# Decays from a transposed broadcast column, with the mask applied on GpSimd, in a gated DeltaNet layer

## The chip, the core and the metric

The kernel runs on one core of a Trainium2 chip. The core has five engines that each take their instructions in program order and wait for one another by semaphores: TensorE (PE, with its weight loads shown as PEld), VectorE (DVE), ScalarE (ACT), GpSimd (POOL) and SyncE (SP), which here issues the large loads. SBUF is the on-chip memory, PSUM the smaller one that PE writes its products to. The metric is device time of one execution, in microseconds; a profile is a separate execution, recorded by the hardware.

## What is computed

One decoder layer over 256 tokens of width 2048: a gated DeltaNet mixer with 16 query/key heads and 32 value heads of 128, then a SwiGLU mixer, each with a modulation before and a layer norm behind it. The part that matters here builds, for each head, the matrix of decays between the positions of a chunk. `gc` is the running sum of the log gates.

```
gc = jnp.cumsum(g, -1)
diff = gc[..., :, None] - gc[..., None, :]
decay = jnp.where(lower, jnp.exp(jnp.where(lower, diff, 0.0)), 0.0)
L = jnp.where(strict, jnp.einsum('bhnid,bhnjd->bhnij', kb, k) * decay, 0.0)
sol = lax.linalg.triangular_solve(L + jnp.eye(C), rhs, left_side=True, lower=True, unit_diagonal=True)
a_qk = jnp.where(lower, jnp.einsum('bhnid,bhnjd->bhnij', q, k) * decay, 0.0)
```

So the products of keys with keys and of queries with keys are multiplied elementwise by exp(gc_i - gc_j), and entries where the key comes after the query are zero. The kernel keeps keys on the partitions and queries along the row, in chunks of 128, which is the same sum cut otherwise.

## The kernel before

All weights stream from device memory in loads of 512 KB. Each load (`raw`) is split into a high part `wh` on ACT (L190) and a low part `wl` on DVE (L191), and three matmuls of 128x512 (L223 to L225) give one product to fp32 precision; there are 6240 such big matmuls. PE works on them from start to end, and the small matmuls and transpositions of the DeltaNet mixer are put between them. The modulation's weights (`mraw`) are partly summed on DVE into `macc` (L272), and PE sums its partitions at L351.

The 32 heads are done in four quarters of eight. A quarter has these steps, all of them short tasks between big matmuls:

- four la tasks (`la_task`, two chunks times two groups of four heads), which make the decays and the masked products `LA`;
- `solve_task`: 62 small DVE operations in a chain (L584, L586) that solve the diagonal blocks, a DVE transposition into `XD` (L588), and products on PE from L600 on;
- two state tasks (`state_task`), which carry the state from the first chunk to the second, end with the products at L685, the sum `oq` on DVE (L686) and squares on ACT (L688);
- the norm of the quarter's output, `fo`: small DVE steps (L715 to L717), a power on POOL (L718), a DVE product (L719). It then scales the outputs `oq` at L795.

One la task works as follows. ACT makes four tiles `dg` that hold the column `gc` of a head in every column, plus `below`, a constant of -1e30 where the key comes after the query (L543). PE transposes them into one PSUM tile `pb` (L547), so that `gc` now runs along the row. ACT takes the exponential with minus `gc` as bias (L551) into `dm`. PE multiplies keys with keys and queries into a second PSUM tile `pk` (L556), and DVE multiplies `pk`, the scale `gsc` and `dm` into `LA` (L561). PSUM tiles `pb` and `pk` come from the pool `gd` with two buffers, which the state and solve tasks share; `dg` and `dm` come from the pool tag `V` with three.

The order of all work is set when the kernel is built. Each task is given a due time in units of some 24 big matmuls by `at`, `spawn` and the `yield` values (GDN, LAGAP, LA1 to LA3, SOLVE, HOP), and a scheduler then writes every engine's queue from these priorities. The engines keep to the queues. A quarter's la tasks begin after the quarter before has ended its state tasks.

Of the kernel before, what the change touches and what calls it, by code (L numbers as in the profile page):

```python
# [8 lines left out]
F32 = mybir.dt.float32  # L9
F32R = mybir.dt.float32r  # L10
I32 = mybir.dt.int32
AF = mybir.ActivationFunctionType
OP = mybir.AluOpType
# [16 lines left out]
def gdn_layer_kernel(ctx: ExitStack, tc: tile.TileContext, x, c, mod_w, mod_b, ln_g, ln_b,  # L30
                     w_gu, w_down, w_in, conv_w, a_log, dt_bias, norm_w, w_out, out):
    nc = tc.nc
# [2 lines left out]
    SPLIT, MOD0, MODEVERY = 10, 30.0, 0.95  # L35
    MGAP, CGAP0, CGAP, CSTEP = 1.5, 1.0, 2.0, 2.3
    CONV, PAIR, SILU = 0.2, 0.4, 2.4
    GDN, LAGAP, LA1, LA2, LA3, SOLVE, HOP = 3.0, 0.5, 0.3, 0.6, 1.5, 5.4, 0.6
    ALONE, MACW, ZW, OW = 1.5, 1.0, 0.1, 0.3


    consts = ctx.enter_context(tc.tile_pool(name="consts", bufs=1))
# [6 lines left out]
    act = nc.scalar.activation  # L49
    tt = nc.vector.tensor_tensor  # L50
    ts = nc.vector.tensor_scalar
    stt = nc.vector.scalar_tensor_tensor
    mm = nc.tensor.matmul
    tr = nc.tensor.transpose
# [35 lines left out]
    def tp():  # L90
        return psum.tile([128, 512], F32, name="tp", tag="tp", bufs=2)

    def gd():
        return psum.tile([128, 512], F32, name="gd", tag="gd", bufs=2)
# [17 lines left out]
    jp = work.tile([128, 128], I32, name="jp", tag="hf", bufs=2)  # L112
    nc.gpsimd.iota(jp, pattern=[[1, 128]], base=0, channel_multiplier=-1)
    ident = consts.tile([128, 128], F32, name="ident")
# [3 lines left out]
    ones = upper[:, 127:128]  # L118
    mhalf = consts.tile([128, 16], F32, name="mhalf")
    nc.vector.memset(mhalf, -0.5)  # L120
    below = consts.tile([128, 128], F32, name="below")
    ts(below, jp, 0.0, -1e30, op0=OP.is_gt, op1=OP.mult)

    pbit = work.tile([128, 1], I32, name="pbit", tag="gw0", bufs=1)
    nc.gpsimd.iota(pbit, pattern=[[0, 1]], base=0, channel_multiplier=1)
# [7 lines left out]
    p = tp()  # L133
# [16 lines left out]
    p = tp()  # L150
# [244 lines left out]
    gp = gp_ctx.__enter__()  # L395
# [6 lines left out]
    gc = consts.tile([128, 2, 32], F32, name="gc")  # L402
    ngc = consts.tile([128, 2, 32], F32, name="ngc")
# [132 lines left out]
    def la_task(q, c, g, sc):  # L536

        kqq, hv, la = kq[q], q * 8, LA[q]
        s0 = c * 8 + g * 4
        dg = gp.tile([128, 4, 128], F32, name="dg", tag="V", bufs=3)  # L540
        for i in range(4):
            h = hv + g * 4 + i
            act(dg[:, i, :], below, AF.Identity, bias=gc[:, c, h:h + 1])  # L543
        yield LA1
        pb = gd()
        for i in range(4):
            tr(pb[:, i * 128:(i + 1) * 128], dg[:, i, :], ident)  # L547
        dm = gp.tile([128, 4, 128], F32, name="dm", tag="V", bufs=3)
        for i in range(4):
            h = hv + g * 4 + i  # L550
            act(dm[:, i, :], pb[:, i * 128:(i + 1) * 128], AF.Exp, bias=ngc[:, c, h:h + 1])  # L551
        yield LA2
        pk = gd()
        for n in range(2):
            nn = g * 2 + n
            mm(pk[:, n * 256:(n + 1) * 256], kqq[:, nn, 0, c * 128:(c + 1) * 128],  # L556
               kqq[:, nn, :, c * 128:(c + 1) * 128], start=True, stop=True)
        for i in range(4):
            h = g * 4 + i
            src = pk[:, (i // 2) * 256:(i // 2 + 1) * 256].rearrange("p (a b) -> p a b", a=2)  # L560
            stt(la[:, s0 + i], src, sc[:, 0, c, h:h + 1], dm[:, i, None, :].to_broadcast([128, 2, 128]),  # L561
                op0=OP.mult, op1=OP.mult)

    def solve_task(q):

# [125 lines left out]
    def gdn(q):  # L691


        while q not in rq2 or q and q - 1 not in state_ends:
            yield 0.2
        hv, rk, rq = q * 8, rk2[q], rq2[q]
        LA[q] = gp.tile([128, 16, 2, 128], F32, name="LA", tag="LA", bufs=1)
        sc = work.tile([128, 2, 2, 8], F32, name="gsc", tag="gsc", bufs=2)
        tt(sc[:, 0], rk, rk, op=OP.mult)
        tt(sc[:, 0], sc[:, 0], beta[:, :, hv:hv + 8], op=OP.mult)  # L700
        tt(sc[:, 1, 0], sc[:, 0, 0], kse[:, hv:hv + 8], op=OP.mult)
        for c in range(2):
            for g in range(2):
                spawn(now[0] + LAGAP * (2 * c + g), la_task(q, c, g, sc))
        yield 3 * LAGAP + LA3
        yield from solve_task(q)
        omq[q] = work.tile([128, 2, 8], F32, name="om", tag="om", bufs=2)
        spawn(now[0] + 0.3, state_task(q, 1, sc))
        yield from state_task(q, 0, sc)
        while state_done.get(q) != 2:  # L710
            yield 0.1
        state_ends.add(q)
        f = work.tile([128, 2, 8], F32, name=f"fo{q}", tag=f"fo{q}", bufs=1)
        t = work.tile([128, 2, 8], F32, name="ft", tag="ft", bufs=1)
        tt(t, rq, rq, op=OP.mult)  # L715
        tt(t, t, omq[q], op=OP.mult)
        ts(t, t, 1.0 / 128.0, NORM_EPS, op0=OP.mult, op1=OP.add)  # L717
        nc.gpsimd.tensor_tensor(f.rearrange("p a b -> p (a b)"), t.rearrange("p a b -> p (a b)"), mhalf, op=OP.pow)  # L718
        tt(f, f, rq, op=OP.mult)  # L719
        fo[q] = f  # L720
# [298 lines left out]
    with tc.tile_pool(name="ph3", bufs=1, reuse_waits="tile") as p3:  # L1019
# [76 lines left out]
        for g in range(4):  # L1096
            if g == 1:
                for i, src in enumerate((ln_g, ln_b)):
                    for gg in range(4):
                        tag, n = ("sg", 2) if i and gg > 1 else ("an", 6)  # L1100
# [32 lines left out]
```

## Time and profile before

| | us |
| --- | --- |
| median of three runs | 1725.89 (1725.24 to 1726.46) |
| profiled execution | 1725.16 |
| its span, first to last instruction | 1723.4 |
| PE busy | 1668.0 (97%) |
| DVE busy | 1139.7 (66%) |
| ACT busy | 882.0 (51%) |
| POOL busy | 61.2 (4%) |

The mean granted clock of TensorE is 0.992 of its full speed. The span is 1.76 us shorter than the execution's own time; changes are counted against the execution's time. The quarters' la stages lie from about 250 to 290 us (the first, spread out), then near 400 to 414, 530 to 545 and 658 to 672 us; the ends of the solves at 351.9, 485.2, 609.5 and 725.0 us. The out-projection and the SwiGLU mixer fill the rest. A busy share is an average over the span; what an engine holds up is read from the rows near one wait.

### The profile page before, as it was taken

How to read it: one execution, taken by the hardware profiler on the slowest of the kernel's cores; microseconds unless marked ns; L12 is line 12 of the kernel's file. 1: busy time of each engine (PE TensorE's matmuls, PEld its weight loads, DVE VectorE, ACT ScalarE, POOL GpSimd, SP SyncE). 2: the span in 40 equal slices, each digit the busy share in tenths (PEclk: the TensorE clock that was granted, in tenths of full speed). 3: DMA queues.
4: the chain of work that ended last, by engine and by line, in shares of the span. 5: the costliest groups of instructions: out<-in, count | busy, mean ns of one | idle time of the engine just before them, and what ended most of it. 6: DMA issues, size and time to landing. Idle time of an engine off the chain costs nothing.

```text
span 1723.4 us, 23269 instructions
## 1 busy us (share of the span) xinstructions
PE 1668.0 (97%) x8685; PEld 1325.3 (77%) x8685; DVE 1139.7 (66%) x1635; ACT 882.0 (51%) x1430; POOL 61.2 (4%) x66
## 2 busy tenths in 40 slices
PE   5999999999999999999999999999999999999996
PEld 2666778787887878788787788888878887888885
DVE  2466988958966988847776865865467544455455
ACT  2433669769568667564333744444444443433332
POOL 0000000001001000000000000000000000000003
PEclk8999999999999999999999999999999999999998
DMA  9998786535864777747888586886678666756662
GB/s 347 364 338 286 223 283 191 170 112 159 255 204 117 241 251 241 245 147 238 302 278 282 158 270 185 304 268 189 189 246 284 191 185 207 249 192 192 196 193 101
DMA packets 184082, 390.82 MB, mean 227 GB/s; under 512 B 12112, under 2 KB 14592, under 8 KB 182944
## 3 DMA queue, kind: packets, MB, share of 16 engines
q1 hardware_dynamic: 181952, 378.64, 67.7%
q0 software_dynamic: 2016, 10.68, 1.8%
q8 instruction: 68, 1.11, 0.3%
q14 instruction: 46, 0.38, 0.1%
HBM read 385.08 MB, written 4.19 MB: 226 GB/s over the span
## 4 chain that ended last, share of the span: by engine, by line
PE 70%; DVE 12%; DMA 7%; ACT 5%; issue 4%; POOL 1%; SPq 1%; POOLq 0%; DVEq 0%; ACTq 0%
PE pj L223 19%; PE pj L225 19%; PE pj L224 19%; DMA mraw<-in_mod_w_dram 6%; DVE wl L191 5%; ACT wh L190 2%; PE gd L225 1%; PE gd L224 1%; DVE macc L272 1%; DVE cy L470 1%; PE gd L223 1%; DVE X L586 1%; DVE tmp L584 1%; PE tp L311 1%; PE tp L1039 1%
## 5 line engine op out<-in xcount | busy, mean ns | idle before, releaser
L191 DVE TENSOR_TENSOR wl<-raw,wh 128x1024 fp32r<-128x1024 f32 x522 | 635.1, 1222 | 376.7 <-ACT wh L190 374.1
L190 ACT ACTIVATE wh<-raw 128x1024 fp32r<-128x1024 f32 x522 | 552.3, 1061 | 602.4 <-PE pj L225 481.1
L223 PE MATMUL pj<-wh,h2T 128*128 128x512 f32 x704 | 278.2, 395 | 0.0
L225 PE MATMUL pj<-wh,h2T 128*128 128x512 f32 x704 | 276.7, 393 | 0.0
L224 PE MATMUL pj<-wl,h2T 128*128 128x512 f32 x704 | 276.5, 393 | 0.0
L223 PE MATMUL pj<-wh,hT 128*128 128x512 f32 x640 | 256.8, 403 | 0.0
L224 PE MATMUL pj<-wl,hT 128*128 128x512 f32 x640 | 256.5, 401 | 0.1
L225 PE MATMUL pj<-wh,hT 128*128 128x512 f32 x640 | 256.2, 401 | 0.0
L272 DVE SCALAR_TENSOR_TENSOR macc<-mraw,cond,macc 128x1024 f32<-128x1024 f32 x120 | 153.6, 1280 | 54.6 <-DMA mraw<-in_mod_w_dram 53.9
L223 PEld LDWEIGHTS pj<-wh,h2T 128*128 128x128 f32 x704 | 132.8, 189 | 30.5 <-issue 1.6
L225 PEld LDWEIGHTS pj<-wh,h2T 128*128 128x128 f32 x704 | 132.7, 189 | 28.7 <-issue 0.8
L224 PEld LDWEIGHTS pj<-wl,h2T 128*128 128x128 f32 x704 | 132.7, 188 | 27.8 <-issue 0.8
L223 PEld LDWEIGHTS pj<-wh,hT 128*128 128x128 f32 x640 | 120.8, 189 | 26.7 <-issue 3.3
L224 PEld LDWEIGHTS pj<-wl,hT 128*128 128x128 f32 x640 | 120.8, 189 | 24.5 <-DVE wl L191 0.9
L225 PEld LDWEIGHTS pj<-wh,hT 128*128 128x128 f32 x640 | 120.9, 189 | 24.4 <-issue 1.2
L470 DVE SCALAR_TENSOR_TENSOR cy<-tp,cw,cy 128x255 f32<-128x255 f32 (+2 forms) x192 | 86.2, 476 | 1.3 <-ACT cy L466 1.2
L224 PE MATMUL gd<-wl,hT 128*128 128x512 f32 x128 | 51.5, 404 | 1.4 <-DVE wl L191 1.4
L223 PE MATMUL gd<-wh,hT 128*128 128x512 f32 x128 | 49.9, 398 | 2.0 <-DVE part L256 1.1
L225 PE MATMUL gd<-wh,hT 128*128 128x512 f32 x128 | 51.8, 408 | 0.0
L311 PE MATMUL tp<-mraw,cond 128*32 128x256 f32 x368 | 34.9, 464 | 11.4 <-DMA mraw<-in_mod_w_dram 11.4
L223 PE MATMUL pj<-wh,oTc 128*128 128x512 f32 x112 | 43.9, 392 | 0.0
L225 PE MATMUL pj<-wh,oTc 128*128 128x512 f32 x112 | 43.8, 391 | 0.0
(388 smaller groups left out, 2266.3 us busy)
## 6 DMA issues: line engine op xcount, KB each, us to landing
raw<-in_gdn_w_in_dram SPq DMA_DIRECT2D x194, 512.0 KB, 4.6
mraw<-in_mod_w_dram SPq DMA_DIRECT2D x192, 512.0 KB, 5.4
raw<-in_ffn_w_gu_dram SPq DMA_DIRECT2D x176, 512.0 KB, 4.3
raw<-in_ffn_w_down_dram SPq DMA_DIRECT2D x88, 512.0 KB, 4.6
raw<-in_gdn_w_out_dram SPq DMA_DIRECT2D x64, 512.0 KB, 5.1
x<-in_x_dram SPq DMA_DIRECT2D x8, 256.0 KB, 5.9
r<-in_x_dram POOLq DMA_DIRECT2D x2, 1024.0 KB, 5.0
x1s<-r POOLq DMA_DIRECT2D x2, 1024.0 KB, 6.8
```

The lines of the kernel that those rows point to most:

```text
L190: act(hi, raw, AF.Copy)
L191: tt(lo, raw, f32(hi), op=OP.subtract)
L223: mm(ps, sh, wh, start=start, stop=False)
L224: mm(ps, sh, wl, start=False, stop=False)
L225: mm(ps, sl, wh, start=False, stop=stop)
L272: return stt(acc, w, cond[:, k:k + 1], acc, op0=OP.mult, op1=OP.add)
L311: mm(p[32 * j:32 * j + 32, 0:hw], cond[:, k:k + 1].to_broadcast([128, 32]), raw[:, kl, j * hw:(j + 1) * hw], start=(k == 0), stop=(k == KT ...
L470: stt(y[:, o + s:o + 256], p[:, o:o + 256 - s], tap(3 - s, ct + i), y[:, o + s:o + 256], op0=OP.mult, op1=OP.add)
L584: tt(tv, LD[:, j + 1:32, j:j + 1].to_broadcast([128, n, m]), X[:, j, None, 0:m].to_broadcast([128, n, m]), op=OP.mult)
L586: tt(X[:, j + 1:32, 0:m], X[:, j + 1:32, 0:m], tv, op=OP.subtract)
L1039: tr(p[:, i * 256 + t * 128:i * 256 + (t + 1) * 128], nats[j, t][:, (2 * i2 + i) * 128:(2 * i2 + i + 1) * 128], ident)
```

## The change

The la task takes the column `gc[:, c, h]`, broadcast along the row, as the operand of the transposition, so the tiles `dg`, the four ACT copies and the constant `below` go. The two products of keys stand directly behind the transpositions, in the same step of the task; the yields LA1 and LA2 go. ACT copies the whole PSUM tile into `dm` with one operation of 128x512, POOL overwrites the entries above the diagonal with -1e30 by one `affine_select` in place, and ACT takes the four exponentials from SBUF in place. LAGAP, the distance between la tasks in the planner's units, goes from 0.5 to 0.7; the solve's start goes from 3.0 to 3.6 units after the first la task.

```
-    GDN, LAGAP, LA1, LA2, LA3, SOLVE, HOP = 3.0, 0.5, 0.3, 0.6, 1.5, 5.4, 0.6
+    GDN, LAGAP, LA3, SOLVE, HOP = 3.0, 0.7, 1.5, 5.4, 0.6
...
-    below = consts.tile([128, 128], F32, name="below")
-    ts(below, jp, 0.0, -1e30, op0=OP.is_gt, op1=OP.mult)
...
-        dg = gp.tile([128, 4, 128], F32, name="dg", tag="V", bufs=3)
+        pb = gd()
         for i in range(4):
             h = hv + g * 4 + i
-            act(dg[:, i, :], below, AF.Identity, bias=gc[:, c, h:h + 1])
-        yield LA1
-        pb = gd()
-        for i in range(4):
-            tr(pb[:, i * 128:(i + 1) * 128], dg[:, i, :], ident)
-        dm = gp.tile([128, 4, 128], F32, name="dm", tag="V", bufs=3)
-        for i in range(4):
-            h = hv + g * 4 + i
-            act(dm[:, i, :], pb[:, i * 128:(i + 1) * 128], AF.Exp, bias=ngc[:, c, h:h + 1])
-        yield LA2
+            tr(pb[:, i * 128:(i + 1) * 128], gc[:, c, h:h + 1].to_broadcast([128, 128]), ident)
         pk = gd()
         for n in range(2):
             nn = g * 2 + n
             mm(pk[:, n * 256:(n + 1) * 256], kqq[:, nn, 0, c * 128:(c + 1) * 128],
                kqq[:, nn, :, c * 128:(c + 1) * 128], start=True, stop=True)
+        dm = gp.tile([128, 4, 128], F32, name="dm", tag="V", bufs=3)
+        act(dm, pb.rearrange("p (a b) -> p a b", a=4), AF.Copy)
+        nc.gpsimd.affine_select(dm, dm, pattern=[[0, 4], [1, 128]], compare_op=OP.is_ge, fill=-1e30,
+                                base=0, channel_multiplier=-1)
+        for i in range(4):
+            h = hv + g * 4 + i
+            act(dm[:, i, :], dm[:, i, :], AF.Exp, bias=ngc[:, c, h:h + 1])
         for i in range(4):
             h = g * 4 + i
             src = pk[:, (i // 2) * 256:(i // 2 + 1) * 256].rearrange("p (a b) -> p a b", a=2)
             stt(la[:, s0 + i], src, sc[:, 0, c, h:h + 1], dm[:, i, None, :].to_broadcast([128, 2, 128]),
                 op0=OP.mult, op1=OP.mult)
+        return
+        yield
```

The lines of the changed kernel's la task are L541 (transposition), L545 (products of keys), L548 (copy), L549 (select), L553 (exponential) and L557 (LA). L716 there is the power of the norm, L717 its DVE product, L793 the scaling of `oq`.

POOL's queue from the power at the end of the first quarter to that of the third, before (`rn` is the norm of queries and keys, `X` the solve's start):

```order
L718 TENSOR_TENSOR fo_3258<-ft,mhalf 128x16
L509 TENSOR_TENSOR rn<-ss,mhalf 128x8 x2
L576 MEMSET X 128x512
L578 COPY X<-parity 128x16 x2
L718 TENSOR_TENSOR fo_4480<-ft,mhalf 128x16
L509 TENSOR_TENSOR rn<-ss,mhalf 128x8 x2
```

The same place now:

```order
L549 AFFINE_SELECT dm<-dm 128x512
L716 TENSOR_TENSOR fo_3269<-ft,mhalf 128x16
L549 AFFINE_SELECT dm<-dm 128x512 x3
L507 TENSOR_TENSOR rn<-ss,mhalf 128x8 x2
L574 MEMSET X 128x512
L576 COPY X<-parity 128x16 x2
L716 TENSOR_TENSOR fo_4522<-ft,mhalf 128x16
L549 AFFINE_SELECT dm<-dm 128x512 x4
```

The selects of the second quarter stand around the power of the first, one ahead and three behind; all four of the third stand behind the power of the second. In the fourth quarter it is one and three again.

ACT's queue in the la stage of the third quarter, before (`tp,ss` are squares for the norm of keys, `V,om` those of the state task):

```order
L543 ACTIVATE dg<-below,gc 128x128 x3
L688 ACTIVATE V_4419,om<-oq_2000 128x128 x4
L543 ACTIVATE dg<-below,gc 128x128
L190 ACTIVATE wh<-raw 128x1024
L551 ACT_TABLE_LOAD
L551 ACTIVATE dm<-gd,ngc 128x128 x4
L543 ACTIVATE dg<-below,gc 128x128 x4
L190 ACTIVATE wh<-raw 128x1024
L551 ACTIVATE dm<-gd,ngc 128x128 x4
```

The same place now:

```order
L686 ACTIVATE V_4482,om<-oq_1998 128x128 x4
L548 ACTIVATE dm<-gd 128x512
L495 ACTIVATE knat<-tp 128x256 x2
L499 ACTIVATE tp,ss<-tp 128x128
L553 ACT_TABLE_LOAD
L553 ACTIVATE dm<-dm,ngc 128x128
L188 ACTIVATE wh<-raw 128x1024
L553 ACTIVATE dm<-dm,ngc 128x128 x3
L548 ACTIVATE dm<-gd 128x512
L188 ACTIVATE wh<-raw 128x1024
L553 ACTIVATE dm<-dm,ngc 128x128 x4
L548 ACTIVATE dm<-gd 128x512
```

The copy of a task stands behind the exponentials of the task before, where before the exponentials of a task stood between the `dg` copies of the next.

DVE's queue at the start of the second quarter's la stage, before (`fo`, L719, is the product that waits for POOL's power):

```order
L717 TENSOR_SCALAR ft<-ft 128x16
L470 SCALAR_TENSOR_TENSOR cy<-tp,cw_101,cy 128x253
L191 TENSOR_TENSOR wl<-raw,wh 128x1024 x2
L719 TENSOR_TENSOR fo_3258<-fo_3258,rr 128x16
L715 TENSOR_TENSOR ft<-rr 128x16
L795 SCALAR_TENSOR_TENSOR oq_1457<-oq_1457,fo_3258,nat 128x128 x8
L191 TENSOR_TENSOR wl<-raw,wh 128x1024
L561 SCALAR_TENSOR_TENSOR LA<-gd,gsc,dm 128x256 x4
```

The same place now:

```order
L715 TENSOR_SCALAR ft<-ft 128x16
L717 TENSOR_TENSOR fo_3269<-fo_3269,rr 128x16
L713 TENSOR_TENSOR ft<-rr 128x16
L793 SCALAR_TENSOR_TENSOR oq_1455<-oq_1455,fo_3269,nat 128x128 x5
L557 SCALAR_TENSOR_TENSOR LA<-gd,gsc,dm 128x256
L793 SCALAR_TENSOR_TENSOR oq_1455<-oq_1455,fo_3269,nat 128x128 x2
L189 TENSOR_TENSOR wl<-raw,wh 128x1024
L557 SCALAR_TENSOR_TENSOR LA<-gd,gsc,dm 128x256 x3
```

The product that waits for the power now stands directly behind the step that starts it; two `wl` and a `cy` stood between them before. On PE the transpositions and the products of keys of one task are from 2 to 19 big matmuls apart in the last three quarters, and 80 in the first quarter's second task. The whole la stage stands 25 to 36 big matmuls earlier in the second and third quarters, and the first product of the solves (L600) stands 25, 21, 1 and 35 big matmuls earlier than before.

## Rows read from the trace of the kernel before

**Rows 1.** The page's busy line and its chain that ended last.

```profile
PE 1668.0 (97%) x8685; PEld 1325.3 (77%) x8685; DVE 1139.7 (66%) x1635; ACT 882.0 (51%) x1430; POOL 61.2 (4%) x66
...
PE 70%; DVE 12%; DMA 7%; ACT 5%; issue 4%; POOL 1%; SPq 1%; POOLq 0%; DVEq 0%; ACTq 0%
```

**Rows 2.** Timeline of PE: start us, us, engine, line, operation, count, [idle before <-releaser].

```profile
251.84 0.60 PE L547 MATMUL gd<-ident,dg 128*128 128x128 f32 x4
...
252.51 0.39 PE L224 MATMUL pj<-wl,hT 128*128 128x512 f32 x1
...
722.01 0.39 PE L223 MATMUL pj<-wh,hT 128*128 128x512 f32 x1
...
722.92 0.39 PE L224 MATMUL pj<-wl,hT 128*128 128x512 f32 x1
725.03 0.21 PE L600 MATMUL gd<-XD,LA 32*32 32x32 f32 x1 [1.73 <-DVE XD L588]
```

**Rows 3.** Waits of PE's weight loads and matmuls: total us, times, longest us.

```profile
PEld gd L600 <- DVE XD L588: 3.8, 4, 2.1
...
PE tp L351 <- DVE tmp L584: 1.4, 1, 1.4
```

**Rows 4.** Timeline of DVE, five places.

```profile
398.63 2.19 DVE L795 SCALAR_TENSOR_TENSOR oq<-oq,fo,nat 128x128 f32<-128x128 f32 x8
...
491.25 1.29 DVE L272 SCALAR_TENSOR_TENSOR macc<-mraw,cond,macc 128x1024 f32<-128x1024 f32 x1 [2.01 <-DMA mraw<-in_mod_w_dram]
492.45 2.35 DVE L191 TENSOR_TENSOR wl<-raw,wh 128x1024 fp32r<-128x1024 f32 x2
494.72 1.28 DVE L272 SCALAR_TENSOR_TENSOR macc<-mraw,cond,macc 128x1024 f32<-128x1024 f32 x1
...
723.93 1.05 DVE L588 STREAM_TRANSPOSE XD<-X 128x512 f32<-128x512 f32 x1
```

**Rows 5.** Two stretches: length; PE, PEld, DVE, ACT, POOL busy; clock; DMA; GB/s.

```profile
533.00:608.00 75.00, 73.55 (x355) 58.91 (x354) 70.43 (x155) 53.83 (x121) 3.27 (x2) 1.00 0.68 211
658.00:724.00 66.00, 64.33 (x297) 52.62 (x295) 64.59 (x133) 38.23 (x58) 0.00 (x0) 1.00 0.80 256
```

**Rows 6.** Groups by line: busy us, mean ns of one, idle before and its releasers.

```profile
L543 ACT ACTIVATE dg<-below,gc 128x128 f32<-128x128 f32 x64 | 21.3, 406 | 0.0
L551 ACT ACTIVATE dm<-gd,ngc 128x128 f32<-128x128 f32 x64 | 19.0, 372 | 1.2 <-PE gd L547 1.1
L556 PE MATMUL gd<-kq 128*128 128x256 f32 x64 | 18.2, 385 | 1.0 <-DVE LA L561 1.0
L501 ACT ACTIVATE tp<-tp 128x128 f32<-128x128 f32 x64 | 17.2, 269 | 1.4 <-PE tp L494 0.6
L547 PEld LDWEIGHTS gd<-ident,dg 128*128 128x128 f32 x64 | 8.9, 140 | 5.6 <-ACT dg L543 3.3
L644 ACT ACTIVATE V<-gd 128x512 f32<-128x512 f32 x8 | 4.8, 598 | 7.6 <-DVE Vs L643 4.9 <-PE gd L648 2.7
L838 PE MATMUL tp<-ident,ga 128*128 128x128 f32 x32 | 4.6, 276 | 0.1
```

**Rows 7.** Timeline of ACT in the third quarter's la stage.

```profile
528.94 1.28 ACT L551 ACT_TABLE_LOAD   x1
...
532.41 1.06 ACT L190 ACTIVATE wh<-raw 128x1024 fp32r<-128x1024 f32 x1
```

**Rows 8.** Timeline of POOL, five places.

```profile
360.95 0.34 POOL L578 COPY X<-parity 128x16 f32<-128x16 f32 x2
...
493.65 0.53 POOL L576 MEMSET X<- 128x512 f32 x1 [67.16 <-PE gd L610]
494.24 1.83 POOL L578 COPY X<-parity 128x16 f32<-128x16 f32 x2
...
528.17 2.90 POOL L718 TENSOR_TENSOR fo<-ft,mhalf 128x16 f32<-128x16 f32 x1 [32.10 <-DVE ft L717]
...
1708.40 1.59 POOL L1085 TENSOR_TENSOR rr<-rr,l 128x512 f32<-128x512 f32 x1
```

## The prediction

> **What bounds the kernel now.** I read the page's busy line first: TensorE (PE) is busy 97% of the span, VectorE (DVE) 66%, ScalarE (ACT) 51%, GpSimd (POOL) 4%. So what ACT is spared, or what POOL is given, counts only where PE comes to wait for it. The chain of waits says the same: 70% of it is PE, 12% DVE, 5% ACT [rows 1]. A big matmul of 128x512 starts every 0.227 us: four of these steps lie between 722.01 and 722.92 [rows 2]. So every distance on PE can be told in big matmuls.
>
> Second, I read who releases PE. The weight loads of L600, the first product after the triangular solve, wait for XD once in each of the four quarters: 3.8 us in all, 2.1 the longest [rows 3]. The rows around the last of them show how: a big matmul starts at 722.92 and L600 at 725.03 [rows 2], 0.05 us behind the end of XD at 723.93 + 1.05 [rows 4]. Less the usual 0.23, PE loses 1.9 us there. The other three share 1.7 of the 3.8, some 0.57 each, and PE loses about 0.35 in each. So PE and DVE reach the end of each solve together, within a fraction of a microsecond in three of four. The stretches of the last two solves show why: DVE is busy 70.43 of 75 us (94%) and 64.59 of 66 (98%) [rows 5]. In these quarters the second bound is DVE's queue, and what makes DVE idle can come out on PE at L600.
>
> Third, the la stage itself. PE waits there for LA (L556 behind L561) 1.0 us. The weight loads of its transpositions (L547) idle 5.6 us in all, 3.3 of them for dg from ACT [rows 6]; part of this lies under the matmul still running, so PE itself loses between nothing and 3.3, and I take half, 1.6.
>
> **The change part by part.** Span and what lies around it make 1725.16 us in the profiled run; the median is 1725.89, so 0.73 is added at the end.
>
> Off ACT go 64 biased copies, L543, 21.3 us busy. On come 16 copies of 128x512 from PSUM at 0.60, the duration of L644, so 9.6. The 64 exponentials stay; read from SBUF they cost between nothing and 0.034 us more, the difference between L543 (SBUF, 406 ns) and L551 (PSUM, 372) [rows 6], so 0 to 2 us. Net some 10 us off ACT, with no direct worth: ACT is at 51%. The `below` tile on DVE is one 128x128 operation at the start, worth nothing. On PE the number of matmuls stays. L838 transposes a broadcast column, as the new L541 does, in 276 ns [rows 6]; four of the old kind take 0.44 us of the stream, from 251.84 to 252.51 less one step of a big matmul [rows 2], which is less than half of four times 276, since they overlap. I take 0.44 for the new ones too. So PE's work is unchanged, and only waits can move the time.
>
> What changes is the path of one task: transposition, ACT copy, POOL select, four exponentials, four LA products, on three engines that each run in order. The select appears nowhere in the trace. The nearest rows: a memset of 128x512 takes 0.53 on POOL, a sum of two operands of that size 1.59 [rows 8]. It reads and writes one tile, so I take 1.0 and keep 0.5 and 1.6. Sixteen are 16 us (8 to 26) on an engine that is empty, and cost PE nothing unless it waits. What stands ahead of them decides. In the order, POOL has the power of the norm (L718) of the quarter before ahead of three selects in the second and fourth quarters and ahead of all four in the third. That power takes 2.90 us and starts only after the state task's squares and three small DVE steps: 528.17 to 531.07 [rows 8], which is 2.7 to 5.7 us after the last state product in that quarter. Before, no path from la to PE led over POOL. DVE stands at the power as well (L719), and the first LA products stand behind L719, as before. I count from that last product (t = 0) and let PE go on in big matmuls as the new order has them.
>
> Third quarter: the first select runs 5.7 to 6.7. Its exponentials (0.3 each, with a wh of 1.06 among them [rows 7]) end at 9.0. ACT's second Copy stands behind them and ends at 9.6. The second pk takes the buffer that this Copy frees; PE stands there at 7.6, 19 big matmuls after the second transpositions at 3.3. It loses 2.0. The third Copy ends at 12.4, its select at 13.4, its exponentials at 14.5; two squarings (0.27 each [rows 6]) and the fourth Copy end at 15.7; PE wants the fourth pk at 14.9 and loses 0.8. With 0.3 elsewhere: 3.1.
>
> Second quarter: the second Copy stands behind a table load (1.28 [rows 7]), the first exponentials and a wh, and ends at 8.0; PE wants it at 7.2 and loses 0.8. The third transpositions take the buffer that the four LA products of task one free. On DVE these stand behind L719 (7.2 here, as the squares come later), seven oq products at 0.27 (eight took 2.19) and one wl at 1.14 (two of them lie between 492.45 and 494.72) [rows 4], and end at 11.9. PE is there at 9.6 and loses 2.3. Sum 3.1.
>
> Fourth quarter: one select is ahead of the power. The same count gives 0.4 and 0.3, so 0.7 in la. At L600 the order brings PE 34 big matmuls (7.7 us) earlier after la's start, and DVE has three wl and three macc less there, 3 x 1.14 + 3 x 1.20 (a macc lies between 491.25 and 492.45 [rows 4]), so 7.0. DVE falls 0.7 further behind; PE's wait there of 1.9 becomes about 2.5, so 0.6.
>
> First quarter: 80 big matmuls (18 us) between its second transpositions and their pk hide the chain: nothing; the cover gone, it would cost like the second, 3.
>
> Taken away: 1.6 at dg, 1.0 at LA, and two waits of 0.35 at L600, since in the second and third quarters PE now comes later than XD: 3.3. Given back: the wait of 1.4 for DVE at L351 [rows 3], which stands in the third quarter behind la and is covered by PE's delay of 3.1. Sum: 3.1 + 3.1 + 0.7 + 0.6 - 3.3 - 1.4 = +2.8. With selects of 0.5 each of the third quarter's two losses falls by 0.5 and the sum to +1.8; with 1.6 each step of it, three selects deep, grows by 0.6, and the sum reaches about +5.
>
> **A row that no engine's own queue explains.** The two copies of parity on POOL take 0.34 us alone; at 494.24 they took 1.83 and ended, at 496.07, as DVE's macc, which reads two operands in SBUF, ended: 494.72 + 1.28 [rows 4, 8]. The Trainium skill, "SBUF — State Buffer", section "SBUF: two separate sides", says that GpSimd shares a port pair with such DVE operations as an exclusive lock held for the whole instruction, and that the loser blocks. By that rule the trace agrees, as far as this pair of copies goes.
>
> **The rivals.** (a) *The cover holds.* Copy, select and exponentials are done before PE comes. For it: POOL is 96% idle, ACT is lighter by 10 us, and LAGAP sets the tasks 0.2 of the planner's units further apart. Against it: the power ahead of the selects in POOL's queue. Its place is pk of the third quarter, and it holds if the second Copy there is done by 7.6 us. Then only what is taken away counts: -3.3, and up to -5.0 if the dg wait was 3.3 rather than 1.6; I take -3.9, so 1725.89 - 3.9 = 1722.0. (b) *Given back.* The losses come, but ACT and DVE run ahead meanwhile, and PE's later waits for them shrink by as much: about 1726. For it: the chain has 12% DVE and 5% ACT outside PE [rows 1]. Against it: in the solves DVE is full [rows 5] and has no room to run ahead. (c) *POOL is held by DVE.* As at 494.24, each select is held by a wl or macc of 1.2 us and holds the next such one. Of the twelve selects in the last three quarters I count one a quarter on the path: 3 x 1.2 on top of 2.8, so 1725.89 + 6.4 = 1732.3. It is what the rule named above would make of the selects. For it: the 1.83; against it: at most places an LA product, with one operand in PSUM, stands beside the select.
>
> **How the numbers follow.** 1725.16 + 2.8 = 1727.96, and 0.73 for the median: 1728.7. A measurement of this kernel can tell about 0.2%, 3.45 us, from no change: below 1722.4 is faster, above 1729.3 slower. Forecast: 0.45, with +0.8 to +6 (1726.7 to 1731.9) as its own range; the bound lies near its middle, so 0.25 beyond it on the slow side and 0.20 within. Cover: 0.28, of it 0.18 beyond on the fast side, since the removed waits just reach it. Given back: 0.12, all within. POOL held: 0.15, all slower. So faster 0.18, within 0.42, slower 0.40. For the range, the cover's case is cut at 1721.8, which leaves some 0.12 below, and POOL's at 1733.0, which leaves some 0.06 above.
>
> **What would show it.** Right: in the third quarter L718's power runs some 2.9 us on POOL with the first select right behind it, and PE waits about 2 us at the second product of keys for ACT's Copy; in the second quarter it waits about 2 us at the third transpositions for LA. The selects last about 1 us. PE at L600 no longer waits in the second and third quarters, but 2 us or more in the fourth. Wrong: no wait of PE over 0.5 us in la (then the cover held), selects of 2 us or ones that end with a wl (POOL held), or waits in la with a total that stands still (given back).

## The result, and the profile after

The changed kernel takes 1745.82 us (median of 4 runs, 1742.38 to 1750.2), the kernel before 1726.18 in the same comparison (4 runs, 1725.24 to 1729.45): a ratio of 1.0115, interval 1.0095 to 1.0135. It is 19.6 us slower, where the prediction had 2.8 and a range that ended at 1733. The profiled execution of after has a span of 1748.4 us, 25.0 above the one of before, and the readings below are of these two executions.

The page of after, the busy line and the chain, which answer to [rows 1]:

```profile
PE 1677.5 (96%) x8685; PEld 1331.7 (76%) x8685; DVE 1141.9 (65%) x1634; ACT 877.0 (50%) x1384; POOL 73.4 (4%) x82
...
PE 65%; DVE 11%; issue 10%; DMA 8%; ACT 3%; POOL 2%; SPq 1%; POOLq 0%; DVEq 0%; ACTq 0%
```

PE has the same 8685 matmuls and is busy with them 9.5 us longer, which fits the lower clock below; DVE is busy 2.2 us longer. The other 15.5 of the 25.0 us are idle time of PE. To see which waits make it, I take in both kernels the stretch from 240 us to the end of the fourth solve. First, after and then before: length; busy time of PE, PEld, DVE, ACT and POOL, each with its instructions; granted clock; DMA share; GB/s.

```profile
240.00:736.00 496.00, 473.78 (x2865) 381.55 (x2865) 397.54 (x801) 345.14 (x725) 40.21 (x38) 0.99 0.62 194
```

```profile
240.00:725.00 485.00, 476.41 (x2900) 383.67 (x2900) 398.50 (x804) 353.68 (x775) 28.15 (x22) 1.00 0.65 201
```

After reaches this point 11 us later, and with 35 matmuls fewer done, which stand behind the solve now (7.9 us at 0.227 each [rows 2]): 18.9 of the 25.0 have been lost by here. PE's share of it: it is idle 496.00 - 473.78 = 22.2 instead of 8.6, so 13.6 more, and the other 5.3 fit the lower clock, below. DVE has done the same work and is idle 98.5 instead of 86.5, so 12.0 more. DVE's waits in the same stretches say for whom (engine, line, waited for: us in all, times, longest), after first:

```profile
DVE wl L189 <- ACT wh L188: 34.6, 30, 6.0
DVE rr L510 <- POOL rn L507: 9.4, 7, 1.8
...
DVE fo L717 <- POOL fo L716: 8.8, 3, 3.0
```

```profile
DVE wl L191 <- ACT wh L190: 35.2, 28, 7.1
...
DVE fo L719 <- POOL fo L718: 3.8, 2, 3.0
...
DVE rr L512 <- POOL rn L509: 3.1, 3, 1.4
```

The two powers on POOL, that of the output's norm (`fo`) and that of the norm of queries and keys (`rn`), keep DVE waiting 18.2 us instead of 6.9. These 11.3 are nearly all of its 12.0, and the wait for ACT has not grown.

What PE sees of it, its waits over the whole run of after (the answer to [rows 3]; the largest, for DMA, is left out, 10.4 us here and 11.4 in before):

```profile
PE gd L541 <- DVE LA L557: 7.3, 2, 4.5
PE gd L598 <- DVE XD L586: 4.1, 3, 2.0
...
PE tp L527 <- ACT cy L471: 2.8, 2, 2.4
...
PE tp L781 <- DVE oTb L816: 2.0, 1, 2.0
...
PE gd L545 <- ACT dm L548: 1.6, 2, 1.2
PE tp L492 <- DVE X L584: 1.4, 1, 1.4
```

The largest of these is at the third transpositions of an la stage, twice: in the second quarter and, longer, in the fourth. The second quarter's, on PE (start, us, engine, line, operation, count, [idle before]):

```profile
399.17 0.40 PE L222 MATMUL pj<-wl,hT 128*128 128x512 f32 x1
402.38 0.65 PE L541 MATMUL gd<-ident,gc 128*128 128x128 f32 x4 [2.81 <-DVE LA L557]
...
404.33 0.63 PE L222 MATMUL pj<-wl,hT 128*128 128x512 f32 x1
404.76 0.63 PE L223 MATMUL pj<-wh,hT 128*128 128x512 f32 x1
```

The last two rows start 0.43 us apart, where big matmuls start every 0.23. The stretches around it, in the columns of the two above; the granted clock is the third number from the right:

```profile
399.00:402.30 3.30, 0.57 (x3) 0.13 (x1) 3.30 (x9) 2.72 (x5) 0.00 (x0) 1.00 0.05 4
402.30:404.30 2.00, 1.92 (x9) 1.63 (x10) 2.00 (x5) 1.17 (x5) 0.51 (x1) 0.84 0.87 250
404.30:406.30 2.00, 2.00 (x6) 1.58 (x5) 0.99 (x3) 1.94 (x4) 0.13 (x1) 0.50 0.84 222
406.30:409.00 2.70, 2.70 (x14) 2.22 (x14) 0.48 (x1) 0.05 (x1) 0.00 (x0) 0.86 0.09 33
...
676.00:680.00 4.00, 3.98 (x14) 3.18 (x15) 2.66 (x5) 2.46 (x5) 1.73 (x1) 0.59 0.07 7
```

After the wait PE runs a while at 0.50, the lower of its two levels (1.2 GHz), and loses 2.0 x 0.16 + 2.0 x 0.50 + 2.7 x 0.14 = 1.7 us more. The fourth quarter's wait of 4.52 costs 4.0 x 0.41 = 1.6 in the same way (last row).

The same place in the fourth quarter, now on the engine that made PE wait. DVE, from the squares of the norm on:

```profile
668.25 1.28 DVE L270 SCALAR_TENSOR_TENSOR macc<-mraw,cond,macc 128x1024 f32<-128x1024 f32 x1 [1.61 <-DMA mraw<-in_mod_w_dram]
...
669.65 0.17 DVE L715 TENSOR_SCALAR ft<-ft 128x16 f32<-128x16 f32 x1
669.74 1.28 DVE L270 SCALAR_TENSOR_TENSOR macc<-mraw,cond,macc 128x1024 f32<-128x1024 f32 x1
673.81 0.59 DVE L717 TENSOR_TENSOR fo<-fo,rr 128x16 f32<-128x16 f32 x1 [2.79 <-POOL fo L716]
674.32 3.22 DVE L557 SCALAR_TENSOR_TENSOR LA<-gd,gsc,dm 128x256 f32<-128x256 f32 x8
```

And POOL in the second, third and fourth quarters:

```profile
394.17 2.90 POOL L716 TENSOR_TENSOR fo<-ft,mhalf 128x16 f32<-128x16 f32 x1 [1.63 <-DVE ft L715]
...
533.45 2.90 POOL L716 TENSOR_TENSOR fo<-ft,mhalf 128x16 f32<-128x16 f32 x1 [32.71 <-DVE ft L715]
536.31 0.64 POOL L549 TENSOR_SCALAR_AFFINE_SELECT dm<-dm 128x512 f32<-128x512 f32 x1
...
669.91 3.86 POOL L716 TENSOR_TENSOR fo<-ft,mhalf 128x16 f32<-128x16 f32 x1 [4.77 <-DVE ft L715]
673.74 0.63 POOL L549 TENSOR_SCALAR_AFFINE_SELECT dm<-dm 128x512 f32<-128x512 f32 x1
677.43 1.73 POOL L549 TENSOR_SCALAR_AFFINE_SELECT dm<-dm 128x512 f32<-128x512 f32 x1 [3.06 <-ACT dm L548]
```

DVE lets the power start (L715), does one `macc`, and then stands 2.79 us at L717 with eight LA products queued behind it. The power is late as well: the `macc` ahead of L714 had waited 1.61 us for its load, and on POOL the power took 3.86 us instead of 2.90. The third transpositions need the buffer that four of these free; they start at 676.02, having waited 4.52.

### The profile page after: what moved, and what is told of

It is laid out like the page before. It is cut to its first block, busy times and chain, and to the rows that moved or that the text cites. A ratio compares the mean times of both kernels' runs of the same rounds, so it can differ in the third digit from the quotient of the medians.

```text
span 1748.4 us, 23265 instructions
## 1 busy us (share of the span) xinstructions
PE 1677.5 (96%) x8685; PEld 1331.7 (76%) x8685; DVE 1141.9 (65%) x1634; ACT 877.0 (50%) x1384; POOL 73.4 (4%) x82
## 4 chain that ended last, share of the span: by engine, by line
PE 65%; DVE 11%; issue 10%; DMA 8%; ACT 3%; POOL 2%; SPq 1%; POOLq 0%; DVEq 0%; ACTq 0%
PE pj L221 18%; PE pj L223 18%; PE pj L222 18%; DMA mraw<-in_mod_w_dram 6%; DVE wl L189 5%; ACT wh L188 1%; PE gd L223 1%; PE gd L222 1%; PE gd L221 1%; DVE cy L468 1%; DVE tmp L582 1%; DVE X L584 1%; POOL rn L507 1%; PE tp L309 1%; DVE macc L270 1%
## 5 line engine op out<-in xcount | busy, mean ns | idle before, releaser
L309 PE MATMUL tp<-mraw,cond 128*32 128x256 f32 x368 | 36.7, 485 | 10.4 <-DMA mraw<-in_mod_w_dram 10.4
```

The lines of the kernel that those rows point to most:

```text
L309: mm(p[32 * j:32 * j + 32, 0:hw], cond[:, k:k + 1].to_broadcast([128, 32]), raw[:, kl, j * hw:(j + 1) * hw], start=(k == 0), stop=(k == KT ...
```

## The experiments

The comparisons below give the ratio to the kernel before, timed in the same session, with its 95% interval. Before took 1726.18 us beside after, and 1729.02, 1726.25, 1727.26 and 1726.69 beside the four sets. So where times of different sets are subtracted below, the difference by the ratios stands beside it; with four or five runs of each it is sure to some 5 us either way.

**First set: which part of the change?** Three theories. Theory 1: the waits in la that the prediction counted, made by the power ahead of the selects in POOL's queue. Theory 2: the new order of the work, which the planner makes from the new times, whatever the mask is made of. Theory 3: the step over POOL in each task, ACT to POOL to ACT.

*The power behind the selects.* In after, the norm waits 3.0 units more and its power is held behind all selects (which are held in order too):

```
+        if q < NQ - 1:
+            yield 3.0
...
-        nc.gpsimd.tensor_tensor(f..., t..., mhalf, op=OP.pow)
+        tc.keep_in_program_order(nc.gpsimd.tensor_tensor(f..., t..., mhalf, op=OP.pow))
```

> The changed kernel, with the selects and the power of the norm kept in one order on POOL so that the power stands behind all four selects of the quarter; on DVE the product that waits for it then stands behind the LA products too. Theory 1 (the power ahead of the selects and of LA makes PE wait, 2.8 us in the second quarter and 4.5 in the fourth, and each such wait is followed by some 3 us at half the clock): both waits and the slow stretches behind them go, 7.3 + 3.3, so about 1735 us. Theory 2 (the new due times put la and solve elsewhere between the big matmuls, and DVE and PE fall out of step at the solves): it stays at 1743 to 1748. Theory 3 (the step over POOL as such is too long): it stays within 3 us of the changed kernel as well, with waits behind the selects.

Measured: 1746.33 us, 1.0105 [1.0080, 1.0131], no better than after. PE's waits (its largest, those for DMA apart):

```profile
PE pj L222 <- DVE wl L189: 3.6, 3, 1.8
PE tp L492 <- DVE ga L353: 3.6, 1, 3.6
PE tp L349 <- DVE cy L468: 3.4, 1, 3.4
PE gd L598 <- DVE XD L586: 3.2, 4, 1.4
```

The wait of L541 for LA falls from 7.3 us to 0.4, but others stand in its place, all for DVE, and DVE still waits 7.7 us for this power and 8.2 for `rn`. Theory 1, as the whole cause, falls.

*No select.* In after:

```
-        nc.gpsimd.affine_select(dm, dm, ...)
...
-            act(dm[:, i, :], dm[:, i, :], AF.Exp, bias=ngc[:, c, h:h + 1])
+            act(dm[:, i, :], dm[:, i, :], AF.Exp, scale=0.0, bias=gc[:, c, h:h + 1])
```

> The changed kernel without the select on POOL; the exponential takes a scale of 0 so that its values stay finite, so the mask and half of the decay are left out. The ACT copy and the four exponentials from SBUF stay. Theory 1: the power still stands ahead of LA on DVE in the second and third quarters, so it gains less than the kernel with the power behind, some 5 us, to 1741. Theory 2: within 4 us of 1746. Theory 3: it returns to 1726 to 1730.

Measured: 1742.22, 1.0081 [1.0055, 1.0107]. Of the 19.6 us 3.6 go by the times, 5.9 by the ratios. From 240 to 740 us DVE still waits 14.9 us for the powers, and L541 still waits 5.3 for LA.

*The mask on DVE.* In after, Copy and select become one sum on DVE that reads PSUM and adds a constant mask, `below`:

```
-        act(dm, pb.rearrange("p (a b) -> p a b", a=4), AF.Copy)
-        nc.gpsimd.affine_select(dm, dm, ...)
+        tt(dm, pb.rearrange("p (a b) -> p a b", a=4), below[:, None, :].to_broadcast([128, 4, 128]), op=OP.add)
```

> The changed kernel, with ACT copy and POOL select replaced by one DVE addition of a constant mask from PSUM (16 of about 0.65 us on DVE, 10 us in all), so la uses no POOL. Theory 1: the power still stands ahead of LA on DVE, the selects are gone; DVE has 10 us more work in quarters where it is full, so PE waits at L600: 1740 or more. Theory 2: 1740 to 1750. Theory 3: 1726 to 1735.

Measured: 1745.32, 1.0086 [1.0057, 1.0114]. DVE waits 16.5 us for the powers, and the transpositions 6.4 for LA. Theory 3, as the main cause, falls with these two: without the step over POOL most of the time stays.

*Before, with the new distance alone.* In before, one number:

```
-    GDN, LAGAP, ... = 3.0, 0.5, ...
+    GDN, LAGAP, ... = 3.0, 0.7, ...
```

> The kernel before, with LAGAP at 0.7 as in the changed kernel and nothing else, so the la tasks and the solves get other due times and the whole order of that part moves. Theory 1: within 4 us of 1726. Theory 2: it loses at least 6 us, to 1732 or more, with waits at L600 of over 2 us. Theory 3: within 4 us of 1726.

Measured: 1739.61, 1.0063 [1.0042, 1.0085], so +10.6 with no operation of the program changed (the new order has four more table loads on ACT). Its stretch to the end of the fourth solve, and DVE's waits for POOL in it:

```profile
240.00:733.00 493.00, 478.65 (x2895) 385.56 (x2895) 397.13 (x796) 358.37 (x778) 24.78 (x22) 0.99 0.63 196
```

```profile
DVE fo L719 <- POOL fo L718: 9.0, 3, 3.0
...
DVE rr L512 <- POOL rn L509: 7.2, 6, 1.4
```

DVE is idle 493.00 - 397.13 = 95.9, 9.4 more than in before, and waits 16.2 for the powers, 9.3 more than 6.9. This is the sign of after again, in a kernel without its operations. Theory 2 stands, and has a mechanism: the orders differ in what stands on DVE between the step that starts a power and the step that needs it.

**Second set: is it DVE's wait for the powers?** To test that, the power is made short and the order left as it is on every engine. A product in the power's place does that; the norms are then left out.

```
-    nc.vector.memset(mhalf, -0.5)
+    nc.vector.memset(mhalf, 0.005)
...
-        nc.gpsimd.tensor_tensor(..., mhalf..., op=OP.pow)
+        nc.gpsimd.tensor_tensor(..., mhalf..., op=OP.mult)
```

In after:

> The changed kernel with every engine's order kept word for word; the powers of the norms on POOL (four of 128x16 at 2.9 us, eight of 128x8 at 1.6) become products with a small constant, some 0.2 us each, so the norms are left out. Theory 4 (DVE, full in the quarters, stands idle for POOL's powers: 8.8 + 9.4 us in the changed kernel against 3.8 + 3.1 in the one before, because the planner gives a power no more time than a product and no longer happens to put other work between): these waits fall to under 2 us, and the time by the 11 us that they grew by or more, to 1728 to 1736. Theory 2 in its narrow form (PE and DVE are out of step for other reasons): 1740 or more.

In before:

> The kernel before, order kept, with the same powers made products. Theory 4: it has 6.9 us of such waits, part of them where DVE has time, so it gains 2 to 6 us, to 1720 to 1725, and the distance to the changed kernel with short powers falls from 19 to under 10 us. Theory 2: no change, and the distance stays.

In before with LAGAP 0.7:

> The kernel before with LAGAP at 0.7, order kept, with the same powers made products. It waits 9.0 + 7.2 us for powers, 9.3 more than the kernel before. Theory 4: it gains 8 to 14 us, to 1726 to 1732, so most of the 10.6 us that LAGAP alone cost is gone. Theory 2: it stays above 1736.

Measured, in 10 runs each beside 25 of before (1726.25): after 1728.55, 1.0005 [0.9994, 1.0016]; before 1723.5, 0.9976 [0.9961, 0.9990]; the new distance 1726.48, 1.0000 [0.9989, 1.0012]. DVE's waits for POOL in after so changed, 240 to 740 us:

```profile
DVE fo L717 <- POOL fo L716: 0.7, 2, 0.3
...
DVE rr L510 <- POOL rn L507: 0.3, 1, 0.3
```

With the same order and short powers after falls from 1745.82 to 1728.55, by 17.3 (19.0 by the ratios), while before falls by 2.8 (4.1). So 14.5 (14.9) of the 19.6 us are the powers' time under the new order. With the new distance alone, 1.0063 becomes 1.0000. Some 5 us between the two orders (1728.55 against 1723.5) are left with the powers short. Of them 3.0 (4.1) come with the new distance alone (1726.48) and 2.1 (0.9) with the rest of the change, each sure to some 3 us either way.

*The followers on POOL as well.* In after, the steps that read the power's result are moved to POOL, so that DVE needn't stand there:

```
-        tt(f, f, rq, op=OP.mult)
+        nc.gpsimd.tensor_tensor(f, f, rq, op=OP.mult)
```

and the same for the two that follow `rn`.

> The changed kernel with the products that follow a power put on POOL too (fo, rr and ik), so that DVE never waits for a power directly; the planner gives a new order. Theory 4: DVE's waits for POOL fall by 10 us or more, and the time to 1730 to 1738, unless the products that use fo and rr stand close behind and wait instead. Theory 2: 1738 to 1750, as for any other order.

Measured: 1739.99, 1.0080 [1.0059, 1.0101]. The wait moves one step along DVE's queue:

```profile
DVE ft L713 <- POOL fo L716: 7.6, 3, 3.0
DVE gsc L697 <- POOL rr L510: 4.8, 3, 2.1
```

The next task's `ft` takes the buffer that the power still reads.

**Third set: which power, and can it be covered?** In after, only one of the powers is made short, by a constant of its own (`op=OP.mult` with `msmall` in place of `mhalf`): the four of `fo`,

> The changed kernel, order kept, with the four powers of the outputs' norm (fo, 2.9 us) made products with a small constant, so that norm is left out; the eight powers of the keys' and queries' norms stay. All twelve short gave 1728.5 against 1745.8. Theory 4a (the prediction's path: the power of fo ahead of selects and LA is the larger part): PE's waits at the third transpositions (7.3 us) and the slow clock behind them go, 1732 to 1736. Theory 4b (the keys' and queries' norms, 9.4 us of DVE's waits, are the larger part): 1737 to 1742.

or the eight of `rn`:

> The changed kernel, order kept, with the eight powers of the keys' and queries' norms (rn, 1.6 us) made products, so those norms are left out; the powers of fo stay. Theory 4a: 1738 to 1742, PE's waits at the third transpositions stay. Theory 4b: 1731 to 1736. If the two parts add up, the two gains sum to about 17 us.

Measured: 1736.66, 1.0062 [1.0040, 1.0084], and 1738.0, 1.0078 [1.0050, 1.0105]. Against after's 1745.82 that is 9.2 and 7.8 us, together 17.0 of the 17.3 of both; by the ratios it is 9.1 and 6.4, together 15.5 of 19.0. So the two add up within the noise. In the first, the third transpositions wait 0.9 us for LA instead of 7.3; in the second they still wait 6.9. So `fo` makes the wait that the prediction looked at, and `rn`, which the prediction never priced, costs about as much, as far as these intervals tell.

*The product of `fo` later, behind LA.* In after:

```
+        if q < NQ - 1:
+            yield 3.0
+        tc.keep_in_program_order(tt(f, f, rq, op=OP.mult))
```

with the LA products held in order too.

> The changed kernel with nothing left out: the product that waits for fo's power comes 3 units later and is kept behind the LA products on DVE, so DVE goes on with LA while POOL computes the power. The planner gives a new order. Theory 4: DVE's wait for fo in the last three quarters falls from 8.8 us to under 1, the waits for rn stay at 5 to 8, so some 1733 to 1738. If the selects behind the power on POOL are what counts, LA waits for the exponentials instead and it stays above 1742.

Measured: 1740.15, 1.0082 [1.0053, 1.0110], above the range expected. As with the followers, the wait moves to the buffer: `ft` waits for POOL's power 6.0 us, two times.

*Both followers later.* In addition:

```
+        yield 0.8
+        tc.keep_in_program_order(ts(r2, r[...], ...))
```

> As the kernel with the product of fo behind LA, and the products that wait for rn's powers come 0.8 units later and are kept in order with the convolutions' operations on DVE, so that other work stands between power and product there too. Nothing is left out. By the order the work between leaves some 6 us of the powers uncovered in the last three quarters against some 12 in the changed kernel. Theory 4: 1728 to 1736. If it is above 1740, covering the power alone does not help, since the order changed with it.

Measured: 1735.7, 1.0055 [1.0037, 1.0073]. DVE waits 4.1 for `rn` and 6.0 for `fo`, 10.1 instead of 18.2, and the time is 10.1 lower than after's (10.4 by the ratios).

**Fourth set: cover for all.** In after, followers later still (4.0 and 1.2 units) and a buffer of `ft` for each quarter:

```
-        t = work.tile([128, 2, 8], F32, name="ft", tag="ft", bufs=1)
+        t = work.tile([128, 2, 8], F32, name=f"ft{q}", tag=f"ft{q}", bufs=1)
```

> The changed kernel with nothing left out, but with other DVE work in front of every product that waits for a power: fo's 4 units later and behind LA, rr's 1.2 units later and in order with the convolutions, and a tile ft for each quarter, since in the two kernels before this the next quarter's first step of the norm (ft, one buffer) waited for the power instead, 3.0 and 6.0 us. Theory 4, that DVE's idle time for POOL's powers is the cause: those waits fall under 2 us and the time comes near that with short powers, 1726 to 1732. If the selects or the order as such cost more than 6 us beside, it stays at 1734 or more.

The same in before:

> The kernel before with the same three edits, nothing left out. It had 6.9 us of such waits in a lucky order. Theory 4: 1721 to 1728, and the distance to the changed kernel treated alike is what the la task's operations themselves cost, 2 to 7 us as with short powers. Without theory 4, an order that nobody chose: 1730 to 1740, like LAGAP alone.

Measured: 1770.63, 1.0253 [1.0231, 1.0274], and 1744.61, 1.0103 [1.0084, 1.0122]. Neither time came down as theory 4 had it. In the first DVE waits 1.9 us in all for POOL's powers from 240 to 740 us, but PE has a new wait, longer than any so far:

```profile
PE gd L597 <- DVE XD L585: 21.8, 4, 15.5
```

DVE ends the second solve 15.5 us after PE has come for it. That the operations held in a fixed order do this is likely, but not shown. In the second kernel the cover did not come about: DVE waits 6.7 us for the powers, as before does with its 6.9, and the kernel is still 18 us slower. So an order can also cost as much as the change did where these waits are no longer than before. Taking the wait away by force cost more than the wait. No version that keeps the norms came below before.

## Why the prediction was right or wrong

*Right: the direction, and one mechanism.* The power stands ahead of the selects, and the first select of the third quarter runs right behind it (533.45 + 2.90, then 536.31). PE then waits for ACT's Copy at the second products of keys: 1.20 us (at 539.74), where 2.0 was counted; the 0.8 at the fourth did not come, and the selects took 0.64, not 1.0. In the second quarter PE waits at the third transpositions for LA 2.81 us, counted as 2.3. At the first product of the fourth solve it waits 2.0 us, where "2 us or more" stood; but in the third it waits 1.2 us, where none was expected. PE's matmuls are the same.

*Wrong: "DVE stands at the power as well (L719), and the first LA products stand behind L719, as before."* It is not as before. In the second quarter of before, a `cy` and two `wl` stood between the step that starts the power and the product that needs it, some 3 us of work that hid it; they stood in the order quoted ahead of the prediction. In the trace of before they leave DVE no idle time there:

```profile
395.23 0.17 DVE L717 TENSOR_SCALAR ft<-ft 128x16 f32<-128x16 f32 x1
395.31 0.48 DVE L470 SCALAR_TENSOR_TENSOR cy<-tp,cw,cy 128x253 f32<-128x253 f32 x1
395.88 2.55 DVE L191 TENSOR_TENSOR wl<-raw,wh 128x1024 fp32r<-128x1024 f32 x2
398.42 0.18 DVE L719 TENSOR_TENSOR fo<-fo,rr 128x16 f32<-128x16 f32 x1
```

In after nothing stands there, and DVE is idle:

```profile
397.10 0.17 DVE L717 TENSOR_TENSOR fo<-fo,rr 128x16 f32<-128x16 f32 x1 [3.02 <-POOL fo L716]
```

The prediction had said itself that DVE is full in the solves [rows 5] and that what makes it idle can come out on PE. It then used the power's end only to date the LA products of two quarters, and priced the idle time of DVE nowhere: +5.0 for `fo`, and +6.3 for `rn`, which has no term at all. The runs with short powers show the price: 17.3 us come back, 9.2 for `fo` and 7.8 for `rn`, where before gives back 2.8.

*Wrong: the fourth quarter, 0.3 in la for the third transpositions.* They wait 4.52. "One select is ahead of the power" was counted, but not that L717 follows the power's start after one `macc` there as well, nor the `macc` ahead of that start, which waited for its load.

*Wrong: 1.6 taken away at `dg`.* The 3.3 us were idle time of the weight loads. The row of PE itself, in the trace of before, has none:

```profile
L547 PE MATMUL gd<-ident,dg 128*128 128x128 f32 x64 | 15.4, 278 | 0.0
```

Read from PE's rows, the places of the sum come to +8.3 instead of +2.8: the third quarter's second products 1.2 (3.1 for that quarter), the second quarter 2.8 (3.1), the fourth 4.5 (0.7), the first 0.4 (0), the starts of the solves 4.1 - 2.1 = 2.0 (-0.1), `dg` 0.0 (-1.6), LA -1.0 (-1.0), and L351 0.7 - 2.3 = -1.6 (-1.4). The rest of the loss lies at places that the sum did not name, such as L527, L781 and L1037, and in the clock.

*Missing: the clock.* No term of the sum had it. After five of its waits (2.31 us at 241.7, 2.81 at 402.4, 4.52 at 676.0, 1.98 at 736.2, 2.02 at 785.2) after shows a lower clock, some 1.7 us lost each time, 8.6 in all; before shows none from 240 to 790. Over the whole run windows of 4 us add up to 17.1 us lost in after and 14.4 in before, which runs at half clock near 36 us, where after does not. But there both wait for DMA (its share is 1.05 from 28 to 44 us), and PE's busy time with the same matmuls is 9.5 us longer in after. So the clock is nearer 8.6 than 2.7 of the 25 us. With short powers after's order shows a clock of 1.00 from 240 to 790 us, so the falls there are a result of these waits, not a cause beside them.

*The rivals.* (a), the cover holds, and (b), given back, did not happen: the waits in la came and the total rose. (c), POOL held by DVE, is there but small: the power took 3.86 us instead of 2.90 with a `macc` running as it began (669.74 to 671.02), a select 1.73 instead of 0.64 beside a `wl` of 1.21 that starts at 677.45, and another 1.21 beside a `wl` at 281.2. That is 1.0, 1.1 and 0.6 us. Two powers of `rn` were lengthened too, to 2.15 and 2.73 us from 1.64, but so were two in before, to 2.69 and 2.61. The Trainium skill, "SBUF — State Buffer", section "SBUF: two separate sides", says that of a GpSimd operation and a DVE operation with two inputs in SBUF the one that starts first holds the shared ports as a lock for its whole instruction, and that the other blocks. The rows above agree with this, though at 677.4 the two starts are 0.02 us apart, too near to tell which was first. A power that began first does not agree: in before a `macc` began inside one, and neither was lengthened.

```profile
654.92 2.90 POOL L718 TENSOR_TENSOR fo<-ft,mhalf 128x16 f32<-128x16 f32 x1 [34.87 <-DVE ft L717]
655.81 1.28 DVE L272 SCALAR_TENSOR_TENSOR macc<-mraw,cond,macc 128x1024 f32<-128x1024 f32 x1 [0.97 <-DMA mraw<-in_mod_w_dram]
```

So here the power does not hold DVE at the ports, and DVE's loss is its wait for the result. The kernel without any select is only 3.6 us (5.9 by the ratios) faster than after, so this rival's mechanism does not make the 19.6.

*Open.* Some 5 us between the orders of after and before remain when the powers are short, 3.0 of them with the new distance alone. PE's waits in these two kernels differ most at the start of the solves (4.4 us at L598 in after's order, 1.8 at L600 in before's), at L781, for the transposed outputs `oT` (1.2 against none), at L545 (1.0) and L541 (0.8). What makes DVE late there is not shown, and neither is what costs the covered kernels their time. Of the 3.2 us that after waits at L781, 2.0 are gone when the powers are short.

## What to carry to other kernels

Where a planner sets the order, a latency between two engines is hidden by whatever happens to stand between its start and its use; before the numbers of the plan are changed, list each such pair (here the steps around POOL's powers) and read from the new order what is left between them. An engine of 4% busy time can set the time of one that is 94% busy. To find out whether a wait is the cause, shrink the duration of the one operation and keep the order: moving an operation changed the whole order, and three times of five the wait moved along or stayed.

## What the hardware showed

- POOL's power takes 2.90 us for 128x16 and 1.64 for 128x8, so it grows with the length of the row; a select in place over 128x512 takes only 0.64.
- A power that begins while DVE runs a `macc` takes about 1 us longer (3.86 at 669.91 in after). One that begins first takes its 2.90, and a `macc` that begins inside it its usual 1.28 (654.92 and 655.81 in before).
- A wait of PE of some 2 us may or may not be followed by a fall of the clock: that of 2.31 us at 241.7 in after was, that of 2.39 at 438.7 in the same execution was not, and neither was that of 1.73 at 725.03 in before [rows 2].
